# Down projection in seven-of-eight block products, spread between the up projection's chunks

## The chip, the cores and the metric

The kernel runs on one core of a Trainium2 chip. A core has five engines, each with a program of its own that it works through in order: TensorE (PE in the profile, with its weight loads as PEld) multiplies matrices, VectorE (DVE) and ScalarE (ACT) work element by element, GpSimd (POOL) does small operations here and issues some DMAs, SyncE (SP) issues the other DMAs. They meet through semaphores. Data lie in DRAM, in the on-chip memory SBUF (128 partitions), or in the eight accumulation banks of PSUM, 128 x 512 floats each, into which TensorE writes. The metric is the device time in microseconds (us); the time before is 1147.34 us.

## The reference, cut to what matters

One decoder layer over 256 tokens of width 2048 in float32. Attention (16 heads) makes `mix`; then

```python
mix = jnp.concatenate([a_out, b_out], axis=-1) @ w_out[l]
h = layer_norm(DEEPNORM_ALPHA * h + mix, ln1_g[l], ln1_b[l])
u = h @ w_up;  g, val = u[..., :5632], u[..., 5632:]
gc = conv_b + sum(conv_w[j] * gp[:, j:j + S] for j in range(3))   # causal, depthwise; gp is g padded in front
f = (jax.nn.silu(gc) * val) @ w_down                              # 5632 -> 2048
h = layer_norm(DEEPNORM_ALPHA * h + f, ln2_g[l], ln2_b[l])
```

The change concerns the up projection, `f`, and the residual `DEEPNORM_ALPHA * h` that is added to it.

## The kernel before

Every matrix product is made of "split" operands: a float32 operand becomes a high part (ScalarE copies it to the rounded type F32R) and a low part (VectorE subtracts the high part from the operand), and a product is high by high, high by low and low by high, three matmuls into one bank. The function `mm` (line 208) issues every matmul, so all have that line.

Weights come as a `stream` of chunks of 1024 KB, 128 x 2048 floats, into four buffers (`raws`). `load(i)` (line 123) issues the DMA on SyncE's queue six chunks ahead. `split(i, half)` (lines 140 and 141) makes the high and low parts of a half chunk, 1024 columns, into six buffers (`splits`), two to three halves ahead. The order of the work is the order in which the program is written: `begin(i)`, `middle(i)` and lists of callbacks (`at`) put the splits and the evaluation of earlier chunks between the matmuls of chunk `i`.

The up projection has 88 chunks, for each of 44 feature blocks (128 features) one of the gate and one of the value. The first two are made with the normalisation of the attention's output. For each of the other 86, `mm_feature` issues 16 pairs of matmuls, 512 and 256 columns wide (the activations' high and low parts lie side by side), into one of eight banks in turn. ScalarE copies half of the bank out (`added`, line 221) and VectorE adds the other half (222); for the gate follow the convolution (445 to 447) and Silu (448), for the value the product (452). The results of all 44 blocks stay in SBUF (`acts`).

The down projection then has 44 chunks, one per feature block. The output, 256 tokens by 2048 columns, fills the eight banks: two blocks of 128 tokens by four of 512 columns. Per feature block `mm_d` adds eight block products of three matmuls each, one to every bank. `split_act` makes the parts of the activations; of every second chunk the low parts are made by `split_dma` (lines 111 to 113): ScalarE writes the negated operand, and a DMA that GpSimd issues adds the operand to it. The last four feature blocks are multiplied column by column, so that VectorE can add the residual (`z_piece`, lines 399 and 402) and start the normalisation of the first 128 tokens while TensorE works on the others. The residual `z` lies in SBUF all the time; `h_piece` (724, 725) scales it by the first normalisation's gain and offset during the up projection.

Of the kernel before, what the change touches and what calls it, by code (L numbers as in the profile page):

```python
# [11 lines left out]
F32 = mybir.dt.float32  # L12
# [4 lines left out]
P = 128  # L17
# [24 lines left out]
PAIRED_END = 4  # L42


@with_exitstack
def hymba_layer(ctx: ExitStack, tc: tile.TileContext, a: dict):
# [10 lines left out]
    work = pool("work", 2)  # L57
# [22 lines left out]
    for f in range(FT):  # L80
        stream.append(("d", f, 0, a["w_d"][f]))
# [3 lines left out]
    first_d = next(i for i, s in enumerate(stream) if s[0] == "d")  # L85
# [11 lines left out]

    def by_dma(i):

        return first_d + 8 <= i < NS - 12 and (i - first_d) % 2 == 0  # L100

    spare = []

    def split_dma(i):
        if not spare:
            spare.append(keep.tile([P, 2, 2, 2048], F32R, name="spare", tag="t2"))
        hi, lo = (spare[0][:, (i - first_d) // 2 % 2, j] for j in range(2))
        t = loaded.pop(i)
        for half in range(2):
            s = slice(1024 * half, 1024 * (half + 1))  # L110
            ACT.activation(lo[:, s], t[:, s], AF.Copy, scale=-1.0)
            POOL.dma_start(lo[:, s], t[:, s], accum_op=ALU.add)
            ACT.activation(hi[:, s], t[:, s], AF.Copy)
            parts[i, half] = (hi[:, s], lo[:, s])
# [11 lines left out]
    def split(i, half, both=None):  # L126
# [4 lines left out]
        if both is None:  # L131
            hi = splits.tile([P, 1024], F32R, name="hi")
            lo = splits.tile([P, 1024], F32R, name="lo")
        else:
            hi, lo = both[:, half], both[:, 2 + half]
# [15 lines left out]
    x2 = keep.tile([P, KT, 2, S], F32R, name="x2", tag="t2")  # L151
    xh, xl = x2[:, :, 0], x2[:, :, 1]
    z = keep.tile([P, 2, D], F32, name="z")
# [5 lines left out]
    def split_x(k0, k1):  # L159
        t = xraw[:, k0 * S:k1 * S].rearrange("p (k t) -> p k t", t=S)  # L160
        ACT.activation(xh[:, k0:k1], t, AF.Copy)
        DVE.tensor_tensor(xl[:, k0:k1], t, xh[:, k0:k1].bitcast(F32), ALU.subtract)
# [4 lines left out]
    def load_table(n):  # L167
        t = keep.tile([P, S], F32, name=n)
        SP.dma_start(t, a[n])
        cst[n] = t  # L170

    def load_consts():
# [5 lines left out]
        lam4 = keep.tile([P, 4, SUB], F32, name="lam4")  # L178
# [10 lines left out]
    def lambdas():  # L189
        vec, lam4 = cst["vec"], cst["lam4"]  # L190
        pr = keep.tile([P, 2, SUB], F32, name="pr")
# [18 lines left out]
    def mm_feature(dst, i, t2):  # L210

        for k in range(KT):
# [3 lines left out]
            mm(dst, wh, t2[:, k].rearrange("p j t -> p (j t)"), k == 0, False)  # L216
            mm(dst[:, 0:S], wl, t2[:, k, 0], False, k == KT - 1)
# [17 lines left out]
    mh = keep.tile([P, NH, S], F32R, name="mh", tag="ma")  # L235
    ml = keep.tile([P, NH, S], F32R, name="ml", tag="mb")
    vals = {}
    val_all = keep.tile([P, 3, 2, 512], F32, name="val", tag="big")
# [148 lines left out]
    gb = {}  # L387
    stats = {}

    def load_gb(which, both):  # L390
        for j, n in enumerate(("g", "b")):
            t = both[:, j]
            src = a[f"ln{which}_{n}"]
            SP.dma_start(t, bass.AP(tensor=src.tensor, offset=src.offset, ap=[[0, P], [1, D]]))
            gb[n] = t

    def z_piece(t, c, src, ln, w=512, alpha=ALPHA):
        s = slice(c * w, (c + 1) * w)
        DVE.scalar_tensor_tensor(z[:, t, s], z[:, t, s], alpha, src, op0=ALU.mult, op1=ALU.add)  # L399
# [14 lines left out]
    acts = {}  # L414

    def act_of(f):
        key = f // 16
        if key not in acts:
            acts[key] = keep.tile([P, min(16, FT - 16 * key), S], F32, name=f"act{key}", tag=("ma", "mb", "big")[key])
        return acts[key][:, f % 16]  # L420


    def u_bank(f, j):
        return bank[2 * (f % 4) + j]

    def summed(f, j):
        t = work.tile([P, S], F32, name="gu"[j] + "s", tag=f"e{j}", bufs=3)
# [485 lines left out]
```

## Time and profile before

| | before |
|---|---|
| median of 3 runs (lowest, highest) | 1147.34 us (1147.29, 1147.60) |
| profiled execution, first to last instruction (span) | 1146.8 us |
| TensorE busy | 1132.4 us, 99% |
| VectorE / ScalarE / GpSimd busy | 717.6 / 587.1 / 41.9 us |
| read from DRAM | 214.80 MB, 189 GB/s over the span |
| up projection, 86 chunks | from 415.1 us, 5.5 us a chunk |

The profile shows one execution, and its own time is the span. Busy time is what an engine spends in instructions; the idle time of an engine that nobody waits for costs nothing. A group of instructions is shown as line, engine, operation, output and inputs with their shapes, count, then busy time, mean duration in ns, and idle time before it with the instruction that ended it. The chain is followed backwards from the last instruction, at each step to what it waited for. The clock that the profile gives for TensorE is the share of full speed granted.

### The profile page before, as it was taken

To read this page: it belongs to the slowest core of one execution; us is meant where nothing else is said; L and a number is where in the kernel's file an instruction comes from. 1 tells how busy PE (TensorE), PEld (TensorE's weight loads), DVE (VectorE), ACT (ScalarE), POOL (GpSimd) and SP (SyncE) were. 2 spreads that over 40 slices of the span, in tenths; PEclk is the share of its full clock that TensorE was granted. 3 is DMA by queue.
4 is the path that set the end of the run, shared out by engine and by line. 5 is a ranking of instruction groups with operands and counts; after the bars stand their busy time and mean duration, and the time that the engine had idled before them with its cause. 6 is when DMAs were issued, how large, how long until landed. Compare 5 with 4: busy or idle time off the path is not lost.

```text
span 1146.8 us, 15285 instructions
## 1 busy us (share of the span) xinstructions
PE 1132.4 (99%) x5992; PEld 967.0 (84%) x5992; DVE 717.6 (63%) x1159; ACT 587.1 (51%) x919; POOL 41.9 (4%) x51
## 2 busy tenths in 40 slices
PE   9999999999999999999999999999999999999995
PEld 6888888888888898888888888888888888888884
DVE  6895886857745777776666666566666523232566
ACT  6555554544443485454554545554454465654441
POOL 0000000000000000000000000000000011110004
PEclk9999999999999999999999999999999999999998
DMA  9755455455455456555555555555555589999721
GB/s 332 277 220 193 153 179 180 152 182 183 158 177 190 172 219 221 184 187 196 192 196 185 183 188 191 201 191 184 184 187 197 195 211 283 301 271 301 263 103 74
DMA packets 37224, 230.47 MB, mean 201 GB/s; under 512 B 4128, under 2 KB 6048, under 8 KB 11936
## 3 DMA queue, kind: packets, MB, share of 16 engines
q1 hardware_dynamic: 33696, 216.92, 53.0%
q0 software_dynamic: 3456, 12.58, 5.8%
q8 instruction: 47, 0.77, 0.3%
q14 instruction: 25, 0.20, 0.1%
HBM read 214.80 MB, written 2.10 MB: 189 GB/s over the span
## 4 chain that ended last, share of the span: by engine, by line
PE 96%; DVE 2%; DMA 1%; SPq 0%; ACT 0%; POOL 0%; issue 0%; POOLq 0%
PE bank L208 95%; DMA raw<-in_w_v 1%; PE bank L331 0%; DVE st L402 0%; DVE z L399 0%; DVE z L800 0%; PE bank L615 0%; SPq L157 0%; DVE z L796 0%; PE bank L378 0%; SPq L123 0%; POOL rstd L410 0%; ACT hf L618 0%; DVE h L630 0%; DVE z L842 0%
## 5 line engine op out<-in xcount | busy, mean ns | idle before, releaser
L141 DVE TENSOR_TENSOR lo<-raw,hi 128x1024 fp32r<-128x1024 f32 (+1 forms) x370 | 438.5, 1200 | 249.0 <-ACT hi L140 248.3
L140 ACT ACTIVATE hi<-raw 128x1024 fp32r<-128x1024 f32 (+1 forms) x370 | 378.5, 1036 | 246.5 <-PE bank L208 207.6
L208 PE MATMUL bank<-h,hi 128*128 128x512 f32 x1376 | 477.2, 390 | 0.0
L208 PE MATMUL bank<-h,lo 128*128 128x256 f32 x1376 | 388.1, 282 | 0.0
L208 PEld LDWEIGHTS bank<-h,hi 128*128 128x128 f32 x1376 | 258.3, 188 | 53.9
L208 PEld LDWEIGHTS bank<-h,lo 128*128 128x128 f32 x1376 | 260.6, 189 | 0.0
L208 PE MATMUL bank<-x,hi 128*128 128x512 f32 x512 | 181.6, 396 | 0.0
L208 PE MATMUL bank<-x,lo 128*128 128x256 f32 x512 | 144.3, 282 | 0.0
L208 PEld LDWEIGHTS bank<-x,hi 128*128 128x128 f32 x512 | 96.2, 188 | 21.6 <-issue 1.3
L208 PEld LDWEIGHTS bank<-x,lo 128*128 128x128 f32 x512 | 96.9, 189 | 0.2
L208 PE MATMUL bank<-hi,x 128*128 128x512 f32 x256 | 85.6, 404 | 0.2 <-ACT hi L140 0.2
L208 PE MATMUL bank<-lo,ah 128*128 128x512 f32 (+1 forms) x242 | 77.2, 394 | 0.0
L208 PE MATMUL bank<-hi,ah 128*128 128x512 f32 (+1 forms) x242 | 77.0, 393 | 0.0
L208 PE MATMUL bank<-hi,al 128*128 128x512 f32 (+1 forms) x242 | 76.9, 392 | 0.0
L466 DVE TENSOR_TENSOR al<-act,ah 128x256 fp32r<-128x256 f32 x44 | 18.6, 424 | 87.2 <-PE bank L208 66.0
L208 PEld LDWEIGHTS bank<-hi,x 128*128 128x128 f32 x256 | 48.3, 189 | 13.1 <-ACT hi L140 2.0
L445 ACT ACTIVATE gc<-gs,vec 128x256 f32<-128x256 f32 x43 | 25.9, 602 | 58.7 <-DVE gs L222 58.7
L208 PEld LDWEIGHTS bank<-hi,al 128*128 128x128 f32 x242 | 45.6, 188 | 10.6
L208 PEld LDWEIGHTS bank<-lo,ah 128*128 128x128 f32 x242 | 45.7, 189 | 10.5
L208 PEld LDWEIGHTS bank<-hi,ah 128*128 128x128 f32 x242 | 45.5, 188 | 10.5
L208 PE MATMUL bank<-spare,ah 128*128 128x512 f32 x192 | 52.7, 396 | 0.0
L208 PE MATMUL bank<-lo,x 128*128 128x512 f32 x128 | 51.2, 400 | 0.7 <-DVE lo L141 0.7
(129 smaller groups left out, 1002.3 us busy)
## 6 DMA issues: line engine op xcount, KB each, us to landing
raw<-in_w_u SPq DMA_DIRECT2D x88, 1024.0 KB, 4.8
raw<-in_w_d SPq DMA_DIRECT2D x44, 1024.0 KB, 6.8
raw<-in_w_qk SPq DMA_DIRECT2D x32, 1024.0 KB, 4.8
raw<-in_w_o SPq DMA_DIRECT2D x16, 1024.0 KB, 4.8
raw<-in_w_v SPq DMA_DIRECT2D x12, 1024.0 KB, 4.8
spare<-raw POOLq DMA_DIRECT2D x24, 512.0 KB, 9.6
raw<-in_w_v SPq DMA_DIRECT2D x8, 256.0 KB, 4.5
raw<-in_w_v SPq DMA_DIRECT2D x4, 512.0 KB, 8.2
```

What stands on the lines that cost most here:

```text
L140: ACT.activation(hi[:, s], t[:, x:y], AF.Copy)
L141: DVE.tensor_tensor(lo[:, s], t[:, x:y], hi[:, s].bitcast(F32), ALU.subtract)
L208: PE.matmul(out, lhsT, rhs, start=start, stop=stop)
L445: ACT.activation(gc, g, AF.Identity, bias=vec[:, C_CB + f:C_CB + f + 1], scale=w[2])
L466: DVE.tensor_tensor(lo, src, hi.bitcast(F32), ALU.subtract)
```

## The change

The down projection is computed in units. A unit is a pair of feature blocks (256 features) and one half of the output columns (1024): on either side of the product a 2 x 2 arrangement of blocks (2 token blocks by 2 feature blocks, times 2 feature blocks by 2 column blocks). Written out these are eight block products. Here sums and differences of the blocks are formed first (four of the activations, `pair_sums`, four of the weights, in `unit_weights`), seven block products are made (Winograd's form, `TERMS`), each summed over the pairs in a bank of its own, and the four output blocks are sums of the seven banks.

Twenty of the 22 pairs are treated so, in three segments of 5, 8 and 7 pairs; each segment runs through the left column half and then the right one. The last two pairs of the right half use the eight plain products (`PLAIN`), and the last four feature blocks (the "tail") stay outside the pairs, as before. While a segment half is "live", four block products follow each chunk of the up projection (`GAP`); they use banks 0 to 6, and the up projection then has bank 7 alone. By the conditions in the loop the live stretches are the chunks 14 to 31, 41 to 68 and 71 to 87; 35 products are left after the last chunk (87). At the end of a segment half `spill` adds up the seven banks and adds the result, by DMAs that GpSimd issues, to the residual; this now lies in DRAM (`zd`). It is stored there after its scaling, and its place in SBUF holds parts of the weights. Before the end it is read back, into the place of the up projection's activations. The last half's sums are added directly (`last_sums`).

The low part of the second half of every second up chunk from chunk 10 on, and of every chunk from 64 on, is made by a DMA on GpSimd's queue, as are some low parts of the tail and, after the last chunk, of the units. ScalarE copies the whole up bank to SBUF, and VectorE adds the two halves there.

The order is no longer that of the program. From the third chunk of the up projection on, each instruction (or few) is a `Task` with an engine, an estimated duration, and the tasks it needs; rings of buffers add further needs. TensorE's order is given. `order()` works out due times from it, and lays the tasks out engine by engine, each time the one due first among those that can start; the instructions are then issued in the order of the start times so found.

```diff
+SEGMENTS = (5, 8, 7)
+N_PAIRS = sum(SEGMENTS)
+GAP = 4
+LAG = 7
+PLAIN = 2
...
-    def by_dma(i):
-
-        return first_d + 8 <= i < NS - 12 and (i - first_d) % 2 == 0
...
-            ACT.activation(lo[:, s], t[:, s], AF.Copy, scale=-1.0)
-            POOL.dma_start(lo[:, s], t[:, s], accum_op=ALU.add)
-            ACT.activation(hi[:, s], t[:, s], AF.Copy)
...
+        now = 0.0
+        for t in pe_last:
+            t.due = now
+            now += t.dur
...
+        for t in reversed(topo):
+            for s in succ.get(t, ()):
+                t.due = min(t.due, s.due - t.dur - t.lat)
...
+            s, eng = pick
+            mine = sorted((t.due, r, i, t) for i, (t, r) in enumerate(ready.items()) if t.eng == eng)
+            t = None
+            for due, r, _, v in mine:
+                if max(r, s) <= s + 0.05 and not any(
+                        x.due < min(due, s + v.dur) and s + 0.05 < y < s + v.dur for _, y, _, x in mine):
+                    t = v
+                    break
+            if t is None:
+                soon = [(max(r, s), due, i, v) for due, r, i, v in mine if r > s + 0.05]
+                s, _, _, t = min(soon)
+            del ready[t]
+            t.start = s
+            free[eng] = t.start + t.dur
...
+        out.sort(key=lambda t: t.start)
...
+            if by_dma:
+                ACT.activation(lo, raw_of[n][:, s], AF.Copy, scale=-1.0)
+            else:
+                ACT.activation(hi, raw_of[n][:, s], AF.Copy)
+
+        def high():
+            ACT.activation(hl_of[n, x][0], raw_of[n][:, s], AF.Copy)
...
+        t = pe(2.78, fn, split_of[n, x] + (users(up_bank(n)) if x == 0 else []))
...
+        def fn():
+            evs[n] = duo.tile([P, 512], F32, name="ev", bufs=3)
+            ACT.activation(evs[n], bank[b], AF.Copy)
+
+        t = act(512, fn, [pe_last[-1]])
+        use = ev_ring.use(t)
+        bank_user[b] = t
+        t1 = dve(S, lambda: DVE.tensor_tensor(evs[n][:, 0:S], evs[n][:, 0:S], evs[n][:, S:2 * S], ALU.add), [t])
+        use.append(t1)
...
+        for dst, x, y, op in ((4, 3, 1, ALU.add), (3, 2, 3, ALU.subtract), (5, 4, 2, ALU.subtract),
+                              (6, 0, 5, ALU.subtract)):
+            last = [dve(P, lambda dst=dst, x=x, y=y, op=op: one(dst, x, y, op), last)]
+            act_use[q] += last
...
+        t1 = dve(512, sums, [load])
+        s_use = (sp_ring if other else sum_ring).use(t1)
+        t3 = dve(512, lambda: DVE.tensor_tensor(T(1), raw("22"), raw("12"), ALU.subtract), [t1])
+        t2 = dve(512, lambda: DVE.tensor_tensor(T(2), raw("22"), T(0), ALU.subtract), [t1])
+        t4 = dve(512, lambda: DVE.tensor_tensor(T(3), raw("21"), T(2), ALU.subtract), [t2])
+        s_use += [t1, t2, t3, t4]
...
+        ha = act(1024, new_a, [load])
+        a_use = hl_ring.use(ha)
+        la = adma(0.5, low_a, [ha]) if apart else dve(1024, low_a, [ha])
...
+        h1 = act(512, high_1, [load])
+        o_use = one_ring.use(h1)
+        l1 = dve(512, low_1, [h1])
+        o_use += [h1, l1]
+        hb0 = act(1024, lambda: high_b(0), [t1, t3])
...
+        lb0 = dve(1024, lambda: low_b(0), [hb0])
+        hb1 = act(1024, lambda: high_b(1), [t4, t2, hb0])
+        lb1 = dve(1024, lambda: low_b(1), [hb1])
...
+    TERMS = {1: ("11", "1", 0), 2: ("12", "a", 0), 3: ("s4", "a", 1), 4: ("22", "b1", 1), 5: ("s1", "b0", 0),
+             6: ("s2", "b1", 0), 7: ("s3", "b0", 1)}
+    PRODUCTS = (2, 3, 1, 5, 7, 6, 4)
...
+            dst = bank[m - 1]
+            mm(dst, al[:, 0], wh, first, False)
+            mm(dst, al[:, 0], wl, False, False)
+            mm(dst, al[:, 1], wh, False, last)
...
+        k1 = step("c0", "t", 2, [t])
+        o1 = out("c0", 0, 0, [k1])
+        k2 = step("t", "t", 6, [k1])
+        k3 = step("w", "t", 5, [k2], False)
+        k4 = step("w", "w", 3, [k3])
+        o2 = out("w", 0, 1, [k4])
+        k5 = step("t", "t", 7, [k3])
+        k6 = step("c1", "t", 4, [k5])
+        o3 = out("c1", 1, 0, [k6])
+        k7 = step("t", "t", 5, [k6])
+        o4 = out("t", 1, 1, [k7])
+        return [o1, o2, o3, o4]
...
+        st = Task("SP", 0.1, lambda: SP.dma_start(zd.rearrange("t p d -> p t d"), z), last, lat=9.0)
...
+    def by_dma(n, x):
+        return n >= 10 and x == 1 and (n % 2 == 0 or n >= 64)
...
+        if end and m == PRODUCTS[-1]:
+            if h == 0 or ends < N_PAIRS:
+                z_loaded.extend(spill(h))
...
+        up_banks[n] = n if n < 6 else 7 if live or gap or up_banks[n - 1] != 7 else 3
...
+        while queue and gap < GAP:
+            q, h, _, start, _, ends = queue[-1]
+            if not live and n * GAP < GAP * (4 * ends + 1) - 7 * (ends - q - 1) or n < LAG:
+                break
+            assert n >= 4 * q + 5
+            live = True
+            gap += 1
+            if next_product():
+                live = False
+                break
...
+        last["z"] = dma(2, load_z, z_loaded + [last_up], due=(pe_last[-1], 0))
...
+        A = dve(512, lambda: z_add(0, 2, lambda: sp["t"]), [k, z_in], due=(due, 14.0))
+        B = dve(560, lambda: add("t", 6), [A], due=(due, 14.1))
+        C = dve(560, lambda: add("w", 5), [B], due=(due, 14.2))
+        X = dve(512, lambda: z_add(0, 3, lambda: sp["w"]), [C], due=(due, 16.0))
+        E = dve(560, lambda: add("t", 7), [C], due=(due, 16.0))
+        Y = dve(512, lambda: z_add(1, 2, lambda: sp["t"]), [E], due=(due, 24.0))
+        G = dve(560, lambda: add("t", 5), [Y], due=(due, 24.1))
+        H = dve(512, lambda: z_add(1, 3, lambda: sp["t"]), [G], due=(due, 24.2))
...
+    trailing[0] = True
+    load_late()
+    while queue:
+        next_product()
+    for i in range(2, 4):
+        load_tail(i)
+    for x in range(2):
+        for i in range(4):
+            split_tail(i, x, i < 2)
+    split_acts()
+    z_in = last["z"]
+    tail_column(0, 0, True)
+    tail_column(1, 5, True)
+    tail_column(2, 1, False, [last["A"]])
+    tail_column(3, 2, False, [last["X"]])
+    dve(512, lambda: z_add(1, 3, lambda: bank[7]), [last["H"]], due=(pe_last[-1], 0.0))
```

More of the change, by code (lines that the diff above doesn't have):

```diff
@@ L56, in hymba_layer @@
     splits = pool("splits", 6)
[L57 removed]
+    stage = ExitStack()
+    first = stage.enter_context(tc.tile_pool(name="first", bufs=1))
+    work = stage.enter_context(tc.tile_pool(name="work", bufs=2))
     psum = pool("psum", 1, bass.MemoryType.PSUM)
@@ new lines, in plain_weights, with high, low @@
+    def plain_weights(q):
+        load, r_use = load_unit(q, 1)
+        U = lambda: unit[q, 1]
+        unit_use[q, 1], unit_done[q, 1] = {}, {}
+        for j in range(2):
+            s = slice(1024 * j, 1024 * (j + 1))
+            def high(j=j, s=s):
+                U()[j] = splits.tile([P, 2, 1024], F32R, name="hl")
+                ACT.activation(U()[j][:, 0], U()["raw"][:, s], AF.Copy)
+            def low(j=j, s=s):
+                DVE.tensor_tensor(U()[j][:, 1], U()["raw"][:, s], U()[j][:, 0].bitcast(F32), ALU.subtract)
+            t = act(1024, high, [load])
+            use = hl_ring.use(t)
+            use += [t, dve(1024, low, [t])]
+            r_use += use
+            unit_use[q, 1][j], unit_done[q, 1][j] = use, list(use)
@@ new lines, in hymba_layer, with next_product @@
+    queue.reverse()
+    z_loaded = []
+    def next_product():
+        q, h, m, start, end, ends = queue.pop()
+        if m >= 10:
+            if m == 10:
+                plain_parts(q)
+                plain_weights(q)
+            plain_product(q, m - 10)
+            return
+        if m == PRODUCTS[0]:
+            pair_parts(q, h)
+            unit_weights(q, h)
+        product(q, h, m, start, end and (ends < N_PAIRS or h == 0 or m not in (2, 3, 4)))
+        if end and m == PRODUCTS[-1]:
+            if h == 0 or ends < N_PAIRS:
+                z_loaded.extend(spill(h))
+                return True
+            last_sums()
@@ new lines, in z_add, with tail_column, copy @@
+    def z_add(t, c, x):
+        s = slice(c * 512, (c + 1) * 512)
+        DVE.tensor_tensor(zs[2][:, t, s], zs[2][:, t, s], x(), ALU.add)
+    def tail_column(c, b, start, after=()):
+        k = pe(2.78, lambda: mm_tail(bank[b], 0, c, start),
+               [x for i in range(4) for x in tail_split[i, c // 2]] + tail_acts + (users(b) if start else []))
+        bank_user[b] = dve(1000, lambda: z_piece(0, c, bank[b], 2, 512, 1.0), [k, z_in] + list(after), due=(k, 6.0))
+    def copy():
+        sums = zone.tile([P, 4, 512], F32, name="spill")
+        sp["t"], sp["w"] = sums[:, 0], sums[:, 1]
+        ACT.activation(sp["t"], bank[0], AF.Copy)
```

712 lines of the change are left out of this document (551 added, 161 removed).

## The prediction

> **What bounds the kernel now.** I read four views in turn: engine totals and slices, the chain of work that ended last, the stages by window, and the costliest groups by shape.
>
> ```profile
> PE 1132.4 (99%) x5992; PEld 967.0 (84%) x5992; DVE 717.6 (63%) x1159; ACT 587.1 (51%) x919; POOL 41.9 (4%) x51
> DVE  6895886857745777776666666566666523232566
> ACT  6555554544443485454554545554454465654441
> q1 hardware_dynamic: 33696, 216.92, 53.0%
> q0 software_dynamic: 3456, 12.58, 5.8%
> ```
>
> TensorE is busy throughout; VectorE falls from six or seven tenths to two or three in slices 33 to 37, the down projection, so work taken from it there was cheap for VectorE.
>
> ```profile
> 415.06 708.94 PE bank L208 x3744
> ...
> 1124.02 0.70 DVE z L399
> ...
> 1142.62 0.42 DVE z L842
> ```
>
> The chain is one piece of 709 us of matmuls without a break, through the up projection and all but the end of the down projection, and then VectorE's last normalisation. A matmul taken out of that piece shortens the kernel by its own time if nothing else is late. The stages (columns: stage, its length, busy time and count on PE, PEld, DVE, ACT, POOL, clock, DMA share, GB/s):
>
> ```profile
> 560.00:800.00 240.00, 240.00 (x1386) 212.84 (x1385) 148.10 (x194) 119.88 (x174) 0.00 (x0) 1.00 0.54 191
> 1000.00:1100.00 100.00, 100.00 (x431) 80.94 (x430) 38.96 (x44) 51.12 (x63) 7.83 (x9) 1.00 0.87 270
> 57.00:86.00 29.00, 29.00 (x173) 24.78 (x173) 26.28 (x69) 17.53 (x45) 1.41 (x2) 1.00 0.58 218
> 1111.00:1124.00 13.00, 13.00 (x57) 10.53 (x57) 5.71 (x9) 0.00 (x0) 0.00 (x0) 1.00 0.00 0
> ```
>
> Up projection: 1386 matmuls in 240 us, and a chunk has 32, so 5.54 us a chunk. Down projection: 431 in 100 us, 0.232 us each; a block product is three (high by high, high by low, low by high), 0.696 us. The third row matters later: in the attention stage VectorE was 26.28/29 = 91% busy and TensorE lost nothing.
>
> **What is removed.** The seven-product form covers 20 pairs of feature blocks in two column halves, 40 units, less the 2 plain ones: 38 units, one product less in each. 38 x 0.696 = 26.4 us. The other 314 products (38 x 7 + 2 x 8 + 4 x 8) and the 86 chunks keep their matmuls. With nothing late the profiled 1146.8 us become 1120.4.
>
> **What is added, by stage.** A gap of four products follows each up chunk while a segment is live: 5.54 + 4 x 0.696 = 8.32 us a period. A unit lasts 7/4 periods, 14.57 us (1.75 chunks and 7 products). Prices of the instructions:
>
> ```profile
> L141 DVE TENSOR_TENSOR lo<-raw,hi 128x1024 fp32r<-128x1024 f32 x354 | 427.4, 1223 | 242.7 <-ACT hi L140 242.4
> L140 ACT ACTIVATE hi<-raw 128x1024 fp32r<-128x1024 f32 x354 | 368.4, 1054 | 239.5 <-PE bank L208 207.6 <-issue 17.9 <-DMA raw<-in_w_d 9.8
> L445 ACT ACTIVATE gc<-gs,vec 128x256 f32<-128x256 f32 x43 | 25.9, 602 | 58.7 <-DVE gs L222 58.7
> L446 DVE SCALAR_TENSOR_TENSOR gc<-gs,vec,gc 128x255 f32<-128x255 f32 x43 | 20.8, 484 | 28.8 <-ACT gc L445 28.8
> L448 ACT ACTIVATE gc<-gc 128x256 f32<-128x256 f32 x44 | 18.4, 418 | 48.9 <-DVE gc L447 48.9
> L222 DVE TENSOR_TENSOR gs<-bank,gs 128x256 f32<-128x256 f32 x43 | 17.9, 417 | 0.0
> L141 DVE TENSOR_TENSOR lo<-raw,hi 128x512 fp32r<-128x512 f32 x16 | 11.0, 691 | 6.2 <-ACT hi L140 6.0
> L140 ACT ACTIVATE hi<-raw 128x512 fp32r<-128x512 f32 x16 | 10.1, 628 | 7.0 <-DMA raw<-in_w_v 6.7
> L399 DVE SCALAR_TENSOR_TENSOR z<-z,bank 128x512 f32<-128x512 f32 x12 | 8.2, 684 | 9.1 <-PE bank L208 9.1
> L253 ACT ACTIVATE val<-bank 128x512 f32<-128x512 f32 x4 | 2.4, 594 | 0.0
> L325 DVE TENSOR_SCALAR e<-e,rs 128x128 f32<-128x128 f32 x8 | 2.3, 288 | 0.3
> ```
>
> *VectorE, a unit:* four weight sums and the low part of "11" of 512 columns, 5 x 0.691; three low parts of 1024 (a, b0, b1), 3 x 1.223; the low part of the activations, 896 wide, 1.09 by the line through 0.691 and 1.223: 8.21 us. *A chunk:* two halves' low parts less the half that GpSimd's DMA takes in every second chunk, 1.5 x 1.223; the bank sum 0.417; half of two convolution steps and a product, 0.70; four activation sums of 128 a pair, 0.29: 3.24 us. A unit with its 1.75 chunks: 13.88 us of 14.57, or 95%. That is the upper bound, for pieces overlap back to back:
>
> ```profile
> 1103.96 2.35 DVE L141 TENSOR_TENSOR ends<-raw,ends 128x1024 fp32r<-128x1024 f32 x2
> ```
>
> Two take 2.35, so the second adds 1.13 and not 1.22; with 0.08 us off each of some 18 instructions a unit costs 12.5 us, 86%. *ScalarE* likewise: high parts of the unit's weights 3 x 1.054 + 0.628 = 3.79 us, of its activations 0.95, and 3.73 a chunk (splits 2.5 x 1.054, the copy of a whole bank 0.594, half of 0.602 and 0.418): 11.3 us, 77%; from chunk 64 on, where every chunk has a half by DMA, 84%. *DMA:* 53.0% of 1146.8 us for 216.92 MB is 2.94 us for 1024 KB, and 5.8% for 24 accumulates is 2.77 us each; a unit with its chunks takes 2.75 loads and 0.875 accumulates, 10.5 us of 14.57, 72%, and 89% from chunk 64 on, where the down projection ran at 0.87 and TensorE lost nothing. So no engine is over its time as a mean. What I charge is local:
>
> 1. **Hand-offs in the live stretches.** VectorE works in order, at 86 to 95%, with waits for ScalarE (L446: 28.8 us over 43, 0.67 each, 0.59 a unit) that bring the upper bound to 14.47 of 14.57. Every up chunk there uses bank 7, and its copy (0.594, behind at most one 1.054) must be done within the 2.78 us of a gap. Below: nothing, as in the 91% row. Above: 0.35 us in each of the some 35 units that lie between chunks (247 products), 12 us. I take 2, nearer the row.
> 2. **Draining the banks.** A segment half ends with one copy and seven VectorE sums that free banks 0 to 6, 0.594 + 7 x 0.684 = 5.4 us and some hops; in three of five cases the next half starts after one chunk, and its fourth product needs the bank freed last: cover 5.54 + 3 x 0.696 = 7.6 us, in which VectorE also owes a b half of 1.22. Behind a late sum wait the low parts of the next chunk, and on GpSimd's queue the accumulates into DRAM, with the weight halves by DMA behind them. Bounds 0 to 3 us each; I take 0.7 each, 2 us. The half that ends at chunk 83 leaves one product, 0.7 us, as cover for a bank copy of 0.59 and what is ahead of it: 0.7 more (0 to 1.2).
> 3. **The hand-over after the last up chunk.** 4 + 35 products remain, 27.1 us. Only then may the residual (2 MB back from DRAM) and two tail chunks load into the activations' place; two more tail chunks and perhaps one unit are still out: 7 x 2.94 = 20.6 us, and four accumulates 11.1, so 31.7 us of DMA in 27.1. An accumulate issued early takes 2.8 off; the tail's products start on the first chunk and need the fourth 2.1 us later. VectorE owes two units with no chunk between them, 7.0 us for 4.87 of TensorE each (the a part goes by DMA), but the plain units behind them ask 3.4 us for 5.57. Bounds 0 to 4.7 us, I take 2.5.
> 4. **The last normalisation.** Eight sums and a last addition, less the one they replace, put 8 x 0.684 = 5.5 us on VectorE in the four first-token columns; in 1111 to 1124 it had 13.0 - 5.7 = 7.3 us free, but late tail splits (2 x 1.22) come in. Everything behind it is VectorE's chain to the end. Bounds 0 to 3, I take 1.
>
> The residual's store and its reload, the additional reading of ln1's rows and the 20 accumulates of 256 KB are costed at nothing: the store hides behind four chunks of weights in buffers (22 us; without that cover, the 9.3 us below), and no product waits for the accumulates but the reload of point 3. An accumulate into DRAM has no row; from an SBUF one:
>
> ```profile
> z<-in_x SPq DMA_DIRECT2D x1, 2048.0 KB, 9.3
> spare<-raw POOLq DMA_DIRECT2D x24, 512.0 KB, 9.6
> L112 POOL DMA_DIRECT2D spare<-raw x24 | 21.0, 876 | 624.9 <-DVE lo L141 519.1 <-ACT spare L111 104.7 <-PE bank L208 1.0
> ```
>
> half of 2.77 us, times 20 is 28 us of engines over some 450, between nothing and 28 us at worst had TensorE to wait for each; I take nothing. A weight half by DMA needs 1.05 + 0.88 + 9.6 = 11.5 us; six split buffers give it 16.6 us in a live stretch (six of 2.57 a period, less its own 2.76 of use) and 13.9 in a pure up stretch, 2.3 spare. Chunks 69 and 70, two such halves at 2.94 + 2.77 = 5.71 us of DMA in 5.54, are within point 1.
>
> Sum: 1146.8 - 26.4 + 2 + 2 + 0.7 + 2.5 + 1 = 1128.6; the median shown, 1147.34, lies 0.5 above the profiled span, so 1129.
>
> The trace holds one thing that would raise point 3:
>
> ```profile
> 1135.00:1137.00 2.00, 0.15 (x2) 0.00 (x0) 1.86 (x7) 0.00 (x0) 1.79 (x2) 1.00 0.00 0
> 1137.00:1140.00 3.00, 0.00 (x0) 0.00 (x0) 2.53 (x6) 1.48 (x2) 1.74 (x2) 0.86 0.69 279
> 1140.00:1144.00 4.00, 0.00 (x0) 0.00 (x0) 2.94 (x5) 0.00 (x0) 2.36 (x2) 0.50 0.49 185
> ```
>
> The last matmul ended near 1135.2; 0.86 over three us means half clock from about 1139.2, 4 us later. A single stall of 4.7 us, the upper bound, would thus be followed by matmuls at half clock. The Trainium skill (TensorE: Matmul & The Clock Gate, What's actually happening) says that an idle window of about 3.4 us halves the clock and that a busy one of the same length restores it; the trace agrees on the first within 0.6 us, and no run here shows the second. By that rule a stall over the window would cost 1.7 us more, 1130.7 by an estimate from that page; without it the sum stands.
>
> **The rivals.**
>
> *The local waits are large* (points 1 to 4 nearer their upper bounds, 12 + 9 + 4.7 + 3 and 1.2, so up to 30; half of that is 15): 1146.8 - 26.4 + 15 = 1135.4, and 1144 where nine tenths of the gain goes. For it: 95% on an engine in order. Against: the 91% row without loss.
>
> *VectorE becomes the bound, and the kernel is slower.* Place: the live stretches. If VectorE stands 0.25 us at each of the some 12 hand-offs from ScalarE in a unit (it stood 0.67 at L446), a unit takes 13.88 + 3.0 = 16.9 us; over 35 units that is 35 x 2.3 = 81 us lost, 1201. It decides from 26.4/35 = 0.75 us lost a unit, a pace of 15.3 us. With half of the overlap (13.2 + 3.0 = 16.2) it is 57 us lost, 1177. Against it: waits that are seen at 62% load are mostly idleness, which a full queue does not have.
>
> *The GpSimd DMAs starve.* 57 weight halves are to be issued beside a VectorE that is 86 to 95% busy with two-input operations. If an issue of 0.88 us proceeded only in VectorE's pauses, a tenth of the time, it would take some 9 us, the landing 17.6 and the whole 19.5 against 16.6 of lead: 3 us in each of 51 halves, 150 us, 1271. Against: the issue took 0.88 us with VectorE at 39%, where a lock would have shown, and L141 kept its 1.22. The Trainium skill (SBUF - State Buffer, SBUF: two separate sides) describes that starvation for VectorE's two-port modes; the trace has no such issue.
>
> *It does not do what it says:* products would be saved but not in TensorE's time, were the gaps filled by waits for operands of exactly that length. Then within 0.2% of before, 1147.
>
> **How the numbers follow.** Forecast 1129 (from 1121, nothing late, to 1134): 0.58. Large local waits, 1134 to 1144: 0.25. No gain, 1145 to 1149.6: 0.05. VectorE as the bound: 0.09; starvation: 0.03. Range 1121 to 1143: the forecast and most of the second case, 0.8. What a measurement can tell from no change is about 0.2%, 2.3 us. Faster: 0.58 + 0.25 = 0.83; same 0.05; slower 0.12.
>
> **What would show it.** PE instructions 5992 - 114 = 5878; VectorE's busy time near 935 us (717.6 + 312 for 38 units + 23 for pair sums + 29 for 43 drain sums, less 130 for some 107 weight halves and 17 for 40 activation splits no longer made there), over 80% of the span. In the chain, matmuls from 415 to about 1106 with at most 5 us of breaks, the longest at the hand-over; VectorE 86 to 95% in live windows with PE at 100%. Wrong would be PE at 97% or less in a live window with VectorE as releaser, POOL issues well over 1 us, or a tail that ends more than 13 us after the last matmul (before: 11.6).

## The result, and the profile after

The changed kernel takes 1132.45 us (median of 4 runs, 1130.85 to 1135.99); the kernel before, on the same chip, 1147.47 (1147.29 to 1149.17). The ratio is 0.9869, 95% interval 0.985 to 0.9888: faster by 15.0 us. The forecast was 1129, the range 1121 to 1143. The profiled execution of the changed kernel spans 1131.9 us, 14.9 less than before, and the terms below are counted in these two spans; it is one of the two longer ones of the four (1133.67 us), so the terms are those of that execution.

First the page of the kernel after: engine totals, slices of VectorE, queues, and the accumulates' issue on GpSimd.

```profile
PE 1106.6 (98%) x5878; PEld 945.9 (84%) x5878; DVE 900.9 (80%) x1471; ACT 716.6 (63%) x1036; POOL 88.0 (8%) x104
...
DVE  6895886867745787899998768898998687888967
...
q1 hardware_dynamic: 39360, 221.11, 54.6%
q0 software_dynamic: 11088, 35.13, 16.6%
...
L803 POOL DMA_DIRECT2D hl<-raw x51 | 44.6, 875 | 552.8 <-ACT hl L793 386.0
```

The 114 matmuls are gone (5992 to 5878). VectorE rose from 63% to 80%, and an accumulate's issue still takes 0.875 us. TensorE is 98% busy, not 99%, and where it stands is in the view of its waits (who ended the wait; total, times, longest), taken over the up and down projection of the kernel after:

```profile
PE bank L200 <- ACT spill L1379: 4.5, 1, 4.5
PE bank L200 <- ACT ev L899: 3.3, 3, 2.2
PE bank L200 <- DVE bparts L1019: 1.0, 2, 0.8
PE bank L200 <- DVE hl L1112: 0.8, 1, 0.8
PE bank L200 <- ACT bparts L1015: 0.5, 1, 0.5
```

Together 10 us, in few places: 1.3 us near 485 us, at the first live stretch, for the parts of the weight sums (`bparts`); 2.24 us at 912 us for ScalarE's copy of bank 7 (`ev`, line 899 now), and 0.35 and 0.67 more at 984 and 1032; and behind the last up chunk 0.25 us at 1067, 0.76 us at 1089 and 4.49 us at 1096, at the hand-over to the last segment, the longest one behind ScalarE's copy of the first bank of the last half (`spill`, line 1379). By stage, in the columns of the prediction:

```profile
412.00:880.00 468.00, 466.71 (x2523) 404.02 (x2522) 404.09 (x573) 331.39 (x414) 36.67 (x42) 1.00 0.79 246
880.00:915.00 35.00, 32.76 (x165) 27.78 (x164) 22.92 (x35) 24.84 (x32) 4.35 (x5) 0.96 0.93 272
912.00:914.00 2.00, 2.00 (x6) 1.71 (x7) 1.97 (x6) 2.00 (x3) 0.85 (x1) 0.51 0.78 201
914.00:916.00 2.00, 2.00 (x9) 1.72 (x9) 1.86 (x6) 2.00 (x3) 0.36 (x2) 0.64 1.07 385
915.00:1060.00 145.00, 143.98 (x766) 123.62 (x765) 119.60 (x171) 106.75 (x133) 21.82 (x25) 1.00 0.93 262
1060.00:1090.00 30.00, 28.99 (x130) 23.39 (x130) 24.23 (x32) 21.14 (x27) 2.61 (x3) 1.00 0.99 334
1090.00:1108.00 18.00, 13.51 (x52) 10.63 (x51) 14.47 (x22) 9.76 (x14) 1.74 (x2) 0.91 0.66 183
1096.00:1098.00 2.00, 1.98 (x5) 1.60 (x6) 1.93 (x3) 2.00 (x3) 0.00 (x0) 0.59 1.04 197
1098.00:1100.00 2.00, 2.00 (x6) 1.52 (x5) 2.00 (x3) 1.75 (x2) 0.00 (x0) 0.56 0.35 66
```

Up to 880 us, with VectorE 404.09/468 = 86% busy, TensorE loses 1.29 us, all of it at the first live stretch. From then on to the hand-over the DMA share is 0.93 to 0.99 and the long waits fall there. Behind each of the two longest, TensorE's granted clock is 0.51 to 0.64 as a mean of two windows of 2 us: 2 x 0.49 + 2 x 0.36 = 1.7 us lost once more, and 2 x 0.41 + 2 x 0.44 = 1.7 the second time. At a clock of one half, which the windows of 1 us behind the first wait show (0.50), this is 3.4 us of half clock each time.

The chain of waits through the first of them (start, duration, what):

```profile
895.49 1.04 DVE hl L805
896.53 11.96 DMA raw<-in_w_d
...
908.60 0.04 ACT one L1003
...
909.14 0.81 ACT hl L795
...
910.08 1.04 ACT hl L798
911.12 0.31 ACT gc L870
911.43 0.49 ACT ev L899
...
911.97 8.09 PE bank L200 x36
```

Read from the end: TensorE could not start because bank 7 was not copied; the copy stood in ScalarE's program behind four other instructions, and the first of these (`one`, a unit's weights) waited for a load that landed at 908.5. The bank itself had been full since 906.9 us. So a late load stops TensorE by way of an engine that works in order. Why the load was late is in SyncE's waits between 860 and 1060 us: in that time two of its lines stand 170 of 200 us for accumulates that have yet to finish (`hl<-raw`), because a load goes into one of four buffers (`raws`), and an accumulate reads one until it lands.

```profile
SPq L774 <- DMA hl<-raw: 98.6, 14, 11.3
SPq L952 <- DMA hl<-raw: 71.6, 10, 14.6
```

That sum shows how often SyncE stood, not what TensorE lost by it: two of the experiments below have it at 99.6 and 165.6 us, and TensorE waits for nothing in these 200 us.

At the hand-over the chain of the kernel after is of the same kind, a load and then ScalarE's copies of weights, in order, ahead of the bank copy:

```profile
1074.21 15.12 DMA raw<-in_w_d
...
1092.34 0.95 ACT hl L1314
1093.29 1.89 ACT first L1316 x2
1095.18 0.31 ACT tails L1341
1095.49 0.49 ACT spill L1379
...
1096.02 12.85 PE bank L200 x48
```

Finally a gain that the prediction did not have: the up projection begins 2.8 us earlier, at 412.27 instead of 415.06. Two of these come in the output projection of the attention, whose program the change does not touch. In the chain of the kernel before, its matmuls were

```profile
319.58 74.84 PE bank L208 x322
```

and in the chain of the kernel after

```profile
318.86 72.82 PE bank L200 x322
```

The other 0.7 us lie ahead of that stage and are no gain of the change: where it begins differs by as much between executions of one program (the kernel with the two tiles elsewhere, below, began it at 318.09 in one profile and at 319.30 in another).

So the spans add up: 26.4 removed, 2.8 earlier, against 10.05 of waits, 3.4 at half clock, and 0.2 at the end (behind the last matmul 11.9 us, before 11.65): 1146.8 - 26.4 - 2.8 + 10.05 + 3.4 + 0.2 = 1131.25; measured 1131.9.

### The profile page after: what moved, and what is told of

The parts are those of the page before. It is cut to its first block, busy times and chain, and to the rows that moved or that the text cites. A ratio compares the mean times of both kernels' runs of the same rounds, so it can differ in the third digit from the quotient of the medians.

```text
span 1131.9 us, 15587 instructions
## 1 busy us (share of the span) xinstructions
PE 1106.6 (98%) x5878; PEld 945.9 (84%) x5878; DVE 900.9 (80%) x1471; ACT 716.6 (63%) x1036; POOL 88.0 (8%) x104
## 3 DMA queue, kind: packets, MB, share of 16 engines
q0 software_dynamic: 11088, 35.13, 16.6%
## 4 chain that ended last, share of the span: by engine, by line
PE 82%; DMA 9%; DVE 4%; ACT 3%; issue 2%; SPq 0%; POOL 0%; ACTq 0%; POOLq 0%; DVEq 0%
PE bank L200 81%; DMA raw<-in_w_d 3%; DMA raw<-in_w_u 3%; DMA hl<-raw 2%; DMA raw<-in_w_v 1%; ACT hl L795 1%; PE bank L323 0%; DVE st L389 0%; DVE z L386 0%; DVE one L1006 0%; DVE z L1455 0%; DVE hl L805 0%; DVE bparts L1019 0%; ACT ev L899 0%; ACT one L1003 0%
## 5 line engine op out<-in xcount | busy, mean ns | idle before, releaser
L200 PE MATMUL bank<-ha,hl 128*128 128x512 f32 x1376 | 255.0, 338 | 3.3 <-ACT ev L899 3.3
L200 PE MATMUL bank<-hb,hl 128*128 128x512 f32 x1376 | 252.7, 336 | 0.0
L200 PEld LDWEIGHTS bank<-ha,hl 128*128 128x128 f32 x1376 | 216.5, 189 | 35.4 <-ACT ev L899 4.6
L200 PEld LDWEIGHTS bank<-hb,hl 128*128 128x128 f32 x1376 | 211.4, 188 | 27.0
L127 DVE TENSOR_TENSOR hl<-raw,hl 128x1024 fp32r<-128x1024 f32 (+1 forms) x143 | 164.6, 1162 | 69.0 <-ACT hl L126 67.5
L126 ACT ACTIVATE hl<-raw 128x1024 fp32r<-128x1024 f32 (+1 forms) x143 | 143.7, 1009 | 93.0 <-PE bank L200 65.9
L805 DVE TENSOR_TENSOR hl<-raw,hl 128x1024 fp32r<-128x1024 f32 x116 | 140.1, 1220 | 15.9 <-ACT hl L795 15.7
L795 ACT ACTIVATE hl<-raw 128x1024 fp32r<-128x1024 f32 x116 | 120.8, 1052 | 33.5 <-PE bank L200 19.4
L200 PE MATMUL bank<-bparts,aparts 128*128 128x512 f32 x432 | 111.7, 396 | 1.5 <-DVE bparts L1019 1.0
L200 PE MATMUL bank<-xa,hl 128*128 128x512 f32 (+1 forms) x512 | 96.2, 340 | 0.0
L200 PE MATMUL bank<-xb,hl 128*128 128x512 f32 (+1 forms) x512 | 94.7, 337 | 0.0
L793 ACT ACTIVATE hl<-raw 128x1024 fp32r<-128x1024 f32 x51 | 53.8, 1055 | 30.2 <-PE bank L200 30.1
```

What stands on the lines that cost most here:

```text
L126: ACT.activation(hi[:, s], t[:, x:y], AF.Copy)
L127: DVE.tensor_tensor(lo[:, s], t[:, x:y], hi[:, s].bitcast(F32), ALU.subtract)
L200: PE.matmul(out, lhsT, rhs, start=start, stop=stop)
L793: ACT.activation(lo, raw_of[n][:, s], AF.Copy, scale=-1.0)
L795: ACT.activation(hi, raw_of[n][:, s], AF.Copy)
L805: DVE.tensor_tensor(lo, raw_of[n][:, s], hi.bitcast(F32), ALU.subtract)
```

## The experiments

Two questions: what makes the loads late from chunk 64 on, and what the rest of the lost time is. Theory: DMA, by the halves that an accumulate takes in *every* chunk from 64 on. Rival: VectorE, which is relieved by exactly these accumulates.

**Accumulates in every second chunk only.**

```diff
-        return n >= 10 and x == 1 and (n % 2 == 0 or n >= 64)
+        return n >= 10 and x == 1 and n % 2 == 0
```

> The changed kernel, but from chunk 64 on only every second chunk has a half by DMA, as before chunk 64; 12 low parts go back to VectorE. Theory DMA (the stall of 2.24 us before chunk 72, with the half clock behind it, and a part of the 4.49 us at the hand-over come from full DMA engines): the DMA share of 900 to 950 falls from 0.96 to about 0.85, the stall goes, and the time is 1127 to 1129. Theory VectorE (it is the bound in the live stretches): 12 x 1.22 = 14.7 us more for it within some 135 us, 1134 to 1140.

1122.92 us (1122.61 to 1123.15), ratio 0.9776 (0.9762 to 0.9791): below the 1127 to 1129 of the theory, and faster than both kernels; its four runs lie within 0.5 us, those of the changed kernel within 5.1. Its stages:

```profile
880.00:915.00 35.00, 35.00 (x187) 30.15 (x186) 29.72 (x40) 26.08 (x33) 3.09 (x4) 1.00 0.81 262
915.00:1060.00 145.00, 145.00 (x773) 124.71 (x772) 130.51 (x185) 100.19 (x125) 14.42 (x17) 1.00 0.81 240
```

VectorE goes from 82% to 130.51/145 = 90% and TensorE loses nothing there; the share of the DMA engines falls from 0.93 to 0.81. The waits at 912, 984 and 1032 are gone, and so are both stretches at half clock. At the hand-over 1.67 of the 5.25 us of its two long waits remain, so most of what stood there went with the twelve accumulates.

**None on the up chunks.** The tail keeps its four accumulates.

```diff
-        return n >= 10 and x == 1 and (n % 2 == 0 or n >= 64)
+        return False
```

> The changed kernel with all low parts of the up chunks on VectorE, none by DMA: 51 more of 1.13 to 1.22 us, so 13.5 to 14.95 us for VectorE in a unit of 14.57. Theory VectorE, by the upper price: 0.4 us lost in each of 35 units and more at the drains, 1142 to 1150. Theory DMA, by the lower price: VectorE still keeps up, the stall before chunk 72 is gone, 1126 to 1130.

1131.66 us (ratio 0.9853, 0.9838 to 0.9868). The total says little; the stages and one wait say more.

```profile
412.00:880.00 468.00, 467.17 (x2527) 404.44 (x2526) 430.48 (x588) 302.38 (x383) 10.56 (x12) 1.00 0.63 213
...
915.00:1060.00 145.00, 144.17 (x767) 123.73 (x766) 137.37 (x197) 90.68 (x114) 6.07 (x7) 1.00 0.63 196
1060.00:1090.00 30.00, 22.78 (x92) 17.57 (x91) 23.17 (x32) 21.31 (x27) 2.59 (x3) 0.89 0.96 311
```

```profile
PE bank L200 <- DMA hl<-raw: 7.0, 1, 7.0
```

In the live stretch VectorE is 137.37/145 = 94.7% busy and TensorE loses 0.83 us. The rival of the prediction, VectorE as the bound, is thereby refuted up to a load that the changed kernel does not reach. Neither range of the expectation (1126 to 1130, 1142 to 1150) holds the time, because of what follows. What the kernel loses lies behind the last up chunk, for an accumulate of one of the last units: the list here put the residual's reload (issued at 1056.15) ahead of that unit's weights (1059.12), where in the kernel with every second the weights had all been issued by 1053.3. By these times it is a matter of order on one queue, which no run of its own tests; the clock is again reduced behind it (0.89 as the mean of these 30 us).

**Bytes or the held buffer?** An accumulate does two things to the loads: it takes time of the DMA engines, and it keeps its `raws` buffer. Two kernels, both from the changed one. In the first an accumulate moves 128 of 1024 columns, so that it is short and gives the buffer back early. In the second it moves all, but reads another tile, the activations', so that the buffer is free without it. Both leave out part of the low parts, and both keep ScalarE's second copy of these halves and the issue on GpSimd.

```diff
-                POOL.dma_start(lo, raw_of[n][:, s], accum_op=ALU.add)
+                POOL.dma_start(lo[:, 0:128], raw_of[n][:, 1024 * x:1024 * x + 128], accum_op=ALU.add)
```

> The changed kernel, but the 51 accumulates of the up chunks move 128 of their 1024 columns: an eighth of the bytes, with the same instructions on all engines and the same order. It leaves out seven eighths of these low parts (they hold the negated weights), so its output is not the reference's. Theory DMA: the load lands in time, the stall before chunk 72 goes and the hand-over shortens, 1126 to 1129. Theory order (the engines' fixed order would stall anyway): 1132, with the same stalls.

```diff
-                POOL.dma_start(lo, raw_of[n][:, s], accum_op=ALU.add)
+                other = h2[0].rearrange("p k j t -> p (k j t)")[:, 0:1024]
+                POOL.dma_start(lo, other.bitcast(F32), accum_op=ALU.add)
```

> The changed kernel; its 51 accumulates of the up chunks add 1024 columns of the activations' tile instead of the weight chunk, so as many bytes move and all orders stay, but no accumulate holds a weight buffer. It leaves out the true addend of these low parts, so its output is not the reference's. In the changed kernel SyncE's loads between 860 and 1060 us waited 170 us for accumulates to give up their buffer. Theory hold (the load behind an accumulate starts late since it holds one of four weight buffers): the stall of 2.24 us before chunk 72 and its half clock go and the hand-over shortens, 1122 to 1126. Theory bytes (the DMA engines are full from chunk 64 on): 1130 to 1133, with the stalls.

1122.87 us (ratio 0.9773, 0.9757 to 0.9789) and 1123.31 us (ratio 0.9773, 0.9742 to 0.9803): either is enough, and with them ScalarE's copies are ruled out as the cause. The second is the telling one. Its stages:

```profile
880.00:915.00 35.00, 35.00 (x188) 30.12 (x187) 27.41 (x41) 28.62 (x36) 5.71 (x7) 1.00 1.03 300
915.00:1060.00 145.00, 145.00 (x772) 124.75 (x772) 121.72 (x175) 108.87 (x135) 21.38 (x25) 1.00 0.94 271
```

The DMA engines are as full as in the changed kernel (1.03 and 0.94 against 0.93 and 0.93; the view counts a full stretch as slightly above 1), the loads between 880 and 1060 us take longer to land (median 9.2 and 10.6 us against 7.6 and 8.0), and TensorE loses nothing. A full share alone is thus not what stopped the changed kernel. The slices of DMA share over 880 to 912 us, 0.8 us each, show the difference; first the changed kernel, then the one with the other source:

```profile
DMA  9879999999999996999209499989899999999899
```

```profile
DMA  9999999989999999999989899999999999999999
```

In the changed kernel the DMA engines stand almost still from 895 to 897 us, in the midst of a stretch that asks for all of their time, while SyncE's next load waits for a buffer. That is the late load of the chain above, issued directly behind the gap, at 896.53; in the other kernel the same load was issued at 894.83 and the gap isn't there. It then landed in 12.0 us against 8.0, so that of 5.7 us of lateness 1.7 are in the issue and 4.0 in the landing. By SyncE's waits over 883 to 897 us the load ahead of it on the queue, issued at 896.11, had stood 10.1 us for an accumulate, and the late load itself only 0.2 us more, for a low part of VectorE; the chain names that last one. The accumulate had taken just 4.5 us to land, but was issued only at 891.42, behind ScalarE's parts of a load issued at 882.47, and that load had itself stood 7.4 us for an earlier accumulate, by SyncE's waits over 870 to 883 us in the changed kernel:

```profile
SPq L774 <- DMA hl<-raw: 7.4, 1, 7.4
```

So the hold takes the loads' lead away, and in a stretch with a DMA share of 0.93 the lateness was not made up. With short accumulates the hold is still there but ends earlier (4.3 us to landing against 7.3), the DMA share is 0.72 to 0.73, and the up projection's loads land in 4.8 us. That the hold is needed for the stall is shown: without it the same bytes cost nothing. Whether a hold of full length would stall TensorE on an emptier DMA is not, since the short accumulates took away bytes and shortened the hold at once.

**The first live stretch.** In the changed kernel, and in the one with every second, the parts of the first weight sums come late by 1.29 us. They lie in the residual's old place, so its store must land first; the list's figure for that store is 9.0 us, the trace has 7.4. Two kernels, both from the one with every second, change that figure alone.

```diff
-        st = Task("SP", 0.1, lambda: SP.dma_start(zd.rearrange("t p d -> p t d"), z), last, lat=9.0)
+        st = Task("SP", 0.1, lambda: SP.dma_start(zd.rearrange("t p d -> p t d"), z), last, lat=7.0)
```

> e2_every_second, and in the planner the residual's store lasts 7.0 us instead of 9.0 (its landing was measured at 7.4). The first live gap lost 1.29 us to two waits for the b parts; ScalarE stood idle for 3.2 us before them, with the bank copy first in its order. Theory order (the plan puts the parts behind the copy as it takes the store for later than it is): the two waits go, 1121.6. Rival (the parts wait for the store itself): no change, 1122.9.

> The kernel of e2_every_second with one figure of the plan changed: the store of the residual's low parts is planned at 13.0 us instead of 9.0, so that VectorE's scaling and the store are due 4 us earlier; the work is the same. Theory: in e2 the low parts are late at the first live stretch because the store really takes longer than planned (1.29 us of TensorE waits at 484 and 485 us); planned longer it is begun earlier and the waits go, 1121.6 us. Rival: the store can't begin earlier, since the normalisation before it ends late, and the list only moves other work behind it: 1122.9, as e2, or above it.

The second expectation speaks of low parts; what is stored is the scaled residual. The first kernel, with 7.0: 1127.39 us (ratio 0.9809, 0.9773 to 0.9844), the store is issued at 477.2 us instead of 472.5, and the wait grows to 3.43 + 0.47 us. The second, with 13.0: 1124.51 us (ratio 0.9798, 0.9783 to 0.9813), the store is issued at 466.9 and lands at 477.5, and the wait is 1.90 + 0.76 all the same. Neither theory came true, nor the first one's rival of no change. The second one's rival has the time (1122.9 or above) and half of the reason: the store did begin earlier, by 5.6 us, but other work moved behind it. SyncE's and ScalarE's instructions (start, duration, what, idle before and what ended it) in the kernel with 13.0:

```profile
466.90 0.38 SPq L1202 DMA_DIRECT2D zd<-z  x1
469.17 0.53 SPq L952 DMA_DIRECT2D raw<-in_w_d  x1
```

```profile
480.61 1.06 ACT L986 ACTIVATE hl<-raw 128x1024 fp32r<-128x1024 f32 x1 [2.81 <-DMA raw<-in_w_d]
483.42 1.06 ACT L795 ACTIVATE hl<-raw 128x1024 fp32r<-128x1024 f32 x1 [1.74 <-DMA raw<-in_w_u]
...
484.87 1.04 ACT L1015 ACTIVATE bparts<-sums 128x1024 fp32r<-128x1024 f32 x1
```

The weights' load that was issued at 462.72 in the kernel with every second now stands behind the store on SyncE's queue, at 469.17; ScalarE waits for it and for the next, 4.55 us, with `bparts` behind them. The store was earlier and the loads later. In the other direction the store itself was late: it landed at 486.1, and `bparts` followed at 486.6. In the kernel with every second it had landed at 479.9, and ScalarE stood for a bank copy that is ahead in its order, with `bparts` third, at 483.52:

```profile
482.08 0.60 ACT L899 ACTIVATE ev<-bank 128x512 f32<-128x512 f32 x1 [3.21 <-PE bank L200]
```

So 9.0 has the lowest time of the three, though the intervals of 9.0 and 13.0 overlap, and by the traces the 1.29 us come from the order of store, loads and bank copies on two engines, not from the length of the store. No run changes that order alone.

**The hand-over.** In the kernel with every second ScalarE's copies of the tail's weights still stand ahead of the bank copy (1.67 us). Two kernels take such work to VectorE, all of it or half of it; the half is combined with the store at 13.0.

```diff
-            split_tail(i, x, i < 2)
+            split_tail(i, x, False)
```

> e2_every_second, and the tail's low parts all by VectorE: four accumulates (11.1 us of DMA) and four ScalarE copies less at the hand-over, four low parts (4.7 us) more for VectorE. Theory DMA at the hand-over: the 1.67 us before the tail go to under 1, 1121.5 to 1122.5. Rival (VectorE, which has 5.5 us of sums there, becomes late): the chain at the end starts later, 1124 to 1126.

```diff
-            split_tail(i, x, i < 2)
+            split_tail(i, x, i < 2 and x == 1)
```

> e10_store_early with one more edit: of the four low parts behind the last up chunk that ScalarE begins, one of each pair (the second half) goes to VectorE instead of two of two. Theory: half of the work on each engine leaves neither late, so that the 1.2 to 1.7 us of wait ahead of the last segment go and the end behind the last matmul stays at 11.9 us: 1120 to 1121 us. Rival: VectorE is late by the same amount as in e4_tail_on_vector, whose end behind the last matmul was 14.3 us: about 1123 to 1124 us.

All: 1124.16 us (ratio 0.9779, 0.9749 to 0.9809); half: 1124.62 us (ratio 0.9803, 0.9787 to 0.9818). With all of it no wait is left at the hand-over, but the last matmul of that kernel,

```profile
1099.45 7.14 PE L200 MATMUL bank<-hl,tails 128*128 128x512 f32 x42
```

ends at 1106.6 of 1120.9 us: 14.3 us behind it, where the kernel with every second has 11.9. VectorE, late by the low parts that it took over, is late with the normalisation, as the rival had it. The time doesn't tell this kernel from the one with every second (0.9779 and 0.9776, overlapping intervals). Half of it left 0.9 us of wait and 13.0 us of end: neither the theory's 11.9 nor the rival's 14.3, and as slow as the kernel with 13.0 that it was made from (1124.51). What one engine is spared there the other pays. Of the kernels that compute all low parts none measured below the one with every second.

**The 2 us in the output projection.** All its matmuls have the same shapes in both kernels. Two things differ: the change puts the high and low parts of the weights into one tile, and it moves tiles in SBUF, the mixed attention output (`mh`, `ml`) among them. Each was done alone in the kernel before; in the second, those two tiles come from a pool that is laid out behind the weights' parts, and the tiles that take their place after this stage move with them.

```diff
-            hi = splits.tile([P, 1024], F32R, name="hi")
-            lo = splits.tile([P, 1024], F32R, name="lo")
+            both = splits.tile([P, 2, 1024], F32R, name="hl")
+            hi, lo = both[:, 0], both[:, 1]
```

> The kernel before with one edit: the high and the low part of a half chunk lie in one tile (as in the changed kernel) and not in two. In the changed kernel the output projection's 322 recorded matmuls took 72.82 us against 74.84, which no term of the prediction holds. If the place of the two parts does it, that stage is 2.0 us shorter here too and the time about 1145.4. If it is something else (the other tiles that moved when the pools were divided), the stage stays at 74.8 and the time at 1147.4.

```diff
-    mh = keep.tile([P, NH, S], F32R, name="mh", tag="ma")
-    ml = keep.tile([P, NH, S], F32R, name="ml", tag="mb")
+    mh = late.tile([P, NH, S], F32R, name="mh", tag="ma")
+    ml = late.tile([P, NH, S], F32R, name="ml", tag="mb")
...
```

> The kernel before, with the two tiles that hold the attention's output (mh, ml) behind the weights' parts in memory and not ahead of them, as in the changed kernel. If their place makes the output projection's matmuls 2.0 us shorter, the stage of 322 recorded matmuls takes 72.8 us here and 74.8 in the kernel before; if not, 74.8.

> The kernel of e9_late_pool again, timed: the kernel before, with only the stationary tiles of the output projection placed elsewhere in SBUF. Theory: the 2.0 us that this stage lost after the change come from the place of these tiles; the stage again takes 72.8 us and the time is 0.17% below the kernel before, 1145.4 where that is 1147.4. Rival: the single look was chance, the times agree within their interval.

With one tile: 1148.54 us, ratio 0.9997 (0.9987 to 1.0006), the stage at 74.84 us as before; not the cause. With the two tiles elsewhere a single execution took 1145.26 us, and the median of ten is 1146.41 us (1145.31 to 1149.08) against 1148.72, ratio 0.9979 (0.997 to 0.9989). The interval, 0.11 to 0.3% faster, holds the 0.17% that was expected and not zero. The stage in that kernel:

```profile
319.30 72.85 PE bank L209 x322
```

That is the stage of the kernel after, in the kernel before, by the layout of SBUF alone. Groups by shape of one kind of matmul, first before, then with the two tiles elsewhere:

```profile
L208 PE MATMUL bank<-lo,mh 128*128 128x512 f32 x128 | 41.6, 396 | 0.0
```

```profile
L209 PE MATMUL bank<-lo,mh 128*128 128x512 f32 x128 | 40.8, 390 | 0.0
```

Each matmul is 6 ns shorter. Which place matters stays open. With the two tiles (16 x 256 floats each) gone from the first pool, what is laid out behind it, the weights' buffers among them, moves 32 KB nearer the start of each partition, and the matmuls read both; no run moves one without the other.

## Why the prediction was right, point by point

**What bounds, and what is removed: right.** TensorE's chain set the time and still does, and 38 products fewer are 114 matmuls fewer. In the kernel with every second, whose up projection begins at 412.71, 2.35 us earlier than before, the terms close: 1146.8 - 26.4 - 2.35 + 2.96 of waits + 0.2 = 1121.2, measured 1121.4.

**The forecast** stood 3.5 us under the measured time. The charges that it summed are 2 + 2 + 0.7 + 2.5 + 1 = 8.2 us; measured are 14.3 (14.9 gained, of 26.4 + 2.8), of which the points below hold 13.7 and 0.6 has no place. The 2.8 us of an earlier up projection, unforeseen, cancelled almost half of that error; this is luck. Without them the time would have been about 1135, inside the range but in the rival's case of large local waits.

- *Point 1, hand-offs in the live stretches, 2 us:* measured 2.24 + 0.35 = 2.6 us of waits and 1.7 of half clock, 4.3. The mechanism that the text charged, VectorE's hops from ScalarE, cost nothing in 468 us at 86% and, by experiment, 0.83 us at 94.7%: the row of the attention stage, 91% without loss, was the right one to lean on. What did cost is in the last lines of the working: the step "six split buffers give 16.6 and 13.9 us" counted the lead of an accumulate by the buffers it writes, and took a mean DMA share of 0.89 (measured 0.93) as harmless because the down projection ran at 0.87. It did not count the buffer that the accumulate *reads*, of which there are four for all loads.
- *Point 2, draining the banks, 2 us and 0.7 for chunk 83:* the first was nothing, with five segment halves drained behind one chunk or more; the second was 0.67.
- *Point 3, the hand-over, 2.5 us with bounds 0 to 4.7:* measured 0.25 + 0.76 + 4.49 and 1.7 of half clock, 7.2. This is the most mis-sized term, and 5.5 of it in waits alone is above its upper bound. Of its two reasons the DMA sum is borne out (a share of 0.99 over 1060 to 1090 us), and lateness brought from the stretch before came on top (3.58 of the 5.25 us of the two long waits went with the twelve accumulates of every second chunk from 65 on); what was not named is that ScalarE's copies of the tail's weights stand ahead of the bank copy, where the text looked at VectorE's debt.
- *Point 4, the last normalisation, 1 us:* 0.2.
- *Costed at nothing:* the twenty accumulates into DRAM and the reload cost nothing that a wait names, but the reload (17.5 us to landing) went through the same full DMA engines as the tail's loads, for two of which ScalarE stood 3.90 and 1.03 us, so its share of the hand-over stays open; the residual's store cost 1.29 us, not by the loads behind it as the text weighed, but by the parts that need its place and stand in order on ScalarE.
- *The clock:* the sentence that priced a stall of 4.7 us with 1.7 us more is borne out in size: 1.7 behind a stall of 4.49. The trace of before had half clock 4 us after the last matmul; the page of the Trainium skill (TensorE: Matmul & The Clock Gate, What's actually happening) has an idle window of about 3.4 us. Here 2.24 us of idleness were followed by half clock too, so full idleness over 3.4 us was not needed in these runs; 1.90 us, in the kernel with the store at 13.0, were followed by none. Half clock lasted 3.4 us behind both stalls, which agrees with the busy window of about 3.4 us on that page of the Trainium skill.

**The rivals.** VectorE as the bound (1177 to 1201): refuted at 94.7%. GpSimd's DMAs starved (1271): the issue takes 0.875 us beside a VectorE at 80% to 90%, as before. No gain: the time fell by 1.31%. Large local waits (from 1134): as far as the waits go, that is what happened, with 14.3 us, for another reason than "95% on an engine in order".

**What would show it.** 5878 matmuls came as forecast; VectorE's 900.9 us, 79.6% of the span, lie a little below "over 80%" and below the 935 that durations of single instructions had given, and it was 86% busy over 412 to 880 us but 82% from 915 on, where 86 to 95% had been named; matmuls to 1108.87 in the chain where 1106 was forecast, the longest break, 4.49 us, at the hand-over; the end 11.9 us behind the last matmul. One of the signs for wrong came in part: 32.76/35 = 94% in the stretch 880 to 915, with ScalarE and not VectorE as the releaser.

## What to carry to other kernels

When an operation is moved to a DMA, count the buffers it reads as well as those it writes: a buffer read by a DMA stays taken until the DMA lands, and with four buffers for all loads that showed here as idle DMA engines in a full stretch. ScalarE, working in order, handed the lateness of a load on to the bank copy four instructions behind it, so a wait "for ScalarE" is to be followed back through ScalarE's program to the load. VectorE at 94.7% cost 0.83 us in 145 here; a stall of 2.24 us cost 1.7 us more, for the clock behind it.

## What the runs showed of the hardware that was not expected

- The layout of SBUF (two tiles, and with them the buffers behind them) changed a matmul by 6 ns of 396, and the whole kernel by 0.21% (interval 0.11 to 0.3%).
- Half clock followed idle times of TensorE of 2.24 us and more (2.24, 3.43, 4.49 and 7.01 us in different kernels) and none of 1.90 us or less. In the changed kernel it set in 2.3 us after the last matmul at the first stall (912.04 by a granted clock of 0.51 over 912 to 914) and 4.8 us after it at the second (1096.36 by 0.59 over 1096 to 1098), so the time idle is not all that decides.
- The share of the DMA engines stood at 1.03 over 35 us without a wait on TensorE, in the kernel whose accumulates held no load buffer.
